# Mixer outputs split into high and low parts where they are produced, and the residual added by an identity product on TensorE instead of an addition on GpSimd

## Chip, cores and metric

One core of a Trainium2 chip runs the whole program. The metric is device time in microseconds (us): the median of several runs. TensorE is called PE, VectorE DVE, ScalarE ACT, GpSimd POOL; SP is the engine that issues nearly all DMAs.

## What is computed

One layer of a streaming encoder over 1024 frames of width 1024. Four mixers, each with 256 output channels, share one input projection. Their outputs are concatenated, multiplied by `w_out` and added to the residual `h`, which is `x` here. A gated feed-forward network, a gated embedding and a last norm follow. The reference, cut to the part that the change touches:

```python
hn = rms_norm(h, norm_mix_g[i])
z_a, z_b, z_c, z_d = _split(hn @ w_in[i], [A_COLS, B_COLS, C_COLS, D_COLS])
o_a = gmlp_spatial_gating(z_a, ...)
o_b = gated_deltanet(z_b, ...)
o_c = rwkv7_time_mix(z_c, ...)
o_d = conformer_conv(z_d, ...)
h = h + jnp.concatenate([o_a, o_b, o_c, o_d], axis=-1) @ w_out[i]
```

## The kernel before, in words

Large products are made in three pieces. Each float32 operand is split into a high part (a cast to fp32r) and a low part (the operand less its high part), and `mm3` (L136) adds high times high, high times low and low times high in PSUM. A split is an ACT cast (L109) and a subtraction (L112) on DVE, or on POOL for most weights.

The engines' orders are not written out by hand. The Tile framework schedules the instructions by a priority (`tc.cur_priority`) and by the costs it assumes, and fixes one static order for each engine and for SP's queue. An engine takes its instructions in that order: one that waits holds up all behind it.

The stages, by the profile's time, are these. Up to about 205 us come the conformer input and convolution, the gMLP input, and the deltanet inputs (`deltanet_prep`). `gmlp_mix` writes the gMLP output `u` to DRAM as `d_oa`, and `conformer_act` writes the conformer output `cod` as `d_od`, both in float32. Up to about 255 us runs `deltanet_pass1`, a loop over 8 tiles of 128 frames. It is followed by `invert`, a serial chain of small DVE operations (L216 and L220, tiles `X` and `Xt`) that inverts 32x32 blocks, until 291 us. Then come the block products (`blocks`, L1146 and L1148), the 8 deltanet tiles and the preparation of the RWKV mixer. Projections (`mps<-hT,wh`) fill PE in between.

From 440 us the RWKV mixer makes its own matrices (L1025; `LT`, `rCd`), a second `invert` runs on DVE until 493 us, two transposes (L1135, L1137, output `Tn`) follow, and then the block products again. Next come 8 RWKV tiles (`rwkv_tiles`) in a software pipeline. For tile t the operations are L1057 to L1112 and L1166, then the state chain (L867, L884), the transposed output (L1122), the product with `w_out` (`osch`, `oscl`) and the norm for the feed-forward network (L161).

`wout_early` is the low-priority work that PE does beside this. For each tile t of 128 frames it loads the outputs of conformer (m=3) and gMLP (m=0) from DRAM as `oaf`, splits each into `osph` and `ospl` (L109 on ACT, L112 on DVE, at the highest priority, three buffers), and makes for each half of the 1024 columns one PSUM sum of 12 products. This is the staged part. ACT copies the sum into `stg` (L423), and POOL adds the whole tile to `h` (L425), where `x` was loaded. There are 8 such tiles, so 192 staged products and 8 POOL additions of 128x1024. The same is done for deltanet (m=1, 96 products) with a DVE addition instead (L427). The weights of m=1 and m=2 take over the buffers of m=3 and m=0, so the product of any RWKV tile with `w_out` follows the end of the staged part.

Of the kernel before, what the change touches and what calls it, by code (L numbers as in the profile page):

```python
# [9 lines left out]
F32 = mybir.dt.float32  # L10
F32R = mybir.dt.float32r
BF16 = mybir.dt.bfloat16
AF = mybir.ActivationFunctionType
ALU = mybir.AluOpType
# [3 lines left out]
P = 128  # L18
S = 1024
D = 1024  # L20
# [77 lines left out]
class Net:  # L98
# [125 lines left out]
    def body(self):  # L224
        tc, nc, I = self.tc, self.nc, self.i
# [18 lines left out]
            self.eps[v] = e  # L244
        dr = ex.enter_context(tc.tile_pool(name="dr", bufs=1, space=bass.MemoryType.DRAM))
        dt = lambda n, k: dr.tile([P, 2 * k, S], F32, name=n)
        self.d_oa, self.d_ob, self.d_od = dt("d_oa", 1), dt("d_ob", 1), dt("d_od", 1)
        self.d_sg, self.d_c = dt("d_sg", 1), dt("d_c", 3)
        self.d_g = dt("d_g", 2)
        self.d_bk = dr.tile([P, 2, NT, 4, 64], F32, name="d_bk")  # L250
# [107 lines left out]
    def wout_early(self):  # L358
        tc, nc, I = self.tc, self.nc, self.i
        self.base = tc.cur_priority  # L360
        tc.cur_priority = self.base + 100000
        for ms in ((3, 0), (1,)):
            if ms[0] == 1:
                tc.cur_priority = self.base + 10000000
            w = [self.wout_load(m, (nc.vector, None if m == 1 else nc.vector), True) for m in ms]
            for t in range(NT):
                ofs = []
                for m in ms:
                    of = self.wo.tile([P, 2, P], F32, name="oaf", tag="oaf", bufs=2)
                    nc.sync.dma_start(out=of, in_=(self.d_oa, self.d_ob, None, self.d_od)[m][:, :, t * P:(t + 1) * P])  # L370
                    ofs.append(of)
                if ms[0] == 3:
                    nc.sync.dma_start(out=self.h[:, t, :], in_=I["x"][t * P:(t + 1) * P, :])
                for _ in self.wout_tile(t, ofs, w, len(ms) == 2):
                    pass
        tc.cur_priority = self.base
# [31 lines left out]
    def wout_tile(self, t, ofs, ws, staged=False, tag="osp", k="h"):  # L408

        nc = self.nc  # L410
        with self.top():
            os = [self.split(of, tag, [P, 2, P], 3 if tag == "osp" else 2, self.wo if tag == "osp" else self.p2) for of in ofs]
        for half in range(2):
            cs = slice(half * 512, half * 512 + 512)
            ps = self.mps(k)
            n = 2 * len(ofs)
            for j in range(n):
                (oh, ol), w = os[j // 2], ws[j // 2][j % 2]
                self.mm3(ps, oh[:, j % 2, :], ol[:, j % 2, :], w[0][:, cs], w[1][:, cs], j == 0, j == n - 1)
            if staged:  # L420
                if half == 0:
                    stg = self.wo.tile([P, D], F32, name="stg", tag="nxn", bufs=1)
                nc.scalar.copy(out=stg[:, cs], in_=ps)  # L423
                if half == 1:
                    nc.gpsimd.tensor_tensor(out=self.h[:, t, :], in0=stg, in1=self.h[:, t, :], op=ALU.add)  # L425
            else:
                nc.vector.tensor_tensor(out=self.h[:, t, cs], in0=ps, in1=self.h[:, t, cs], op=ALU.add)  # L427
            yield
# [68 lines left out]
    def gmlp_mix(self, u, v_tok, ws, bs):  # L497
        nc = self.nc
        for pr in range(2):
            for half in range(2):  # L500
                ps = self.mps()
                for q in range(4):
                    for hp in range(2):
                        h = 2 * pr + hp
                        nc.tensor.matmul(ps[64 * hp:64 * hp + 64, q * P:(q + 1) * P], v_tok[half][:, q, h * 64:(h + 1) * 64],
                                         ws[:, h, :], start=True, stop=True)
                cs = slice(half * 512, half * 512 + 512)
                t1 = self.dt("gt", [P, 4, P])
                nc.vector.tensor_tensor(out=t1, in0=ps.rearrange("p (n i) -> p n i", i=P),
                                        in1=bs[:, pr:pr + 1, :].broadcast_to([P, 4, P]), op=ALU.add)  # L510
                nc.vector.tensor_tensor(out=u[pr][:, cs], in0=u[pr][:, cs], in1=t1.rearrange("p n i -> p (n i)"), op=ALU.mult)
            nc.sync.dma_start(out=self.d_oa[:, pr, :], in_=u[pr])

    def conformer_in(self):
        tc, nc, I = self.tc, self.nc, self.i
# [43 lines left out]
    def conformer_conv(self, gls):  # L559
# [9 lines left out]
            y.append(yc)  # L569
        return y  # L570

    def conformer_out(self, y, yt, t0):
        nc, I = self.nc, self.i
        for t2 in range(t0, t0 + 2):
            ps = self.mps("a")
            for a in range(2):
                t = 2 * t2 + a
                for c in range(2):
                    nc.tensor.transpose(ps[:, a * 256 + c * P:a * 256 + (c + 1) * P], y[c][:, t * P:(t + 1) * P], self.ident)
            yt.append(self.dt("cyt", [P, 2, G]))  # L580
            self.layernorm_tok(self.ar, ps.rearrange("p (a g) -> p a g", a=2), 2, G, 1e-5, yt[-1])

    def conformer_act(self, yt):
        nc = self.nc
        for c in range(2):
            o = self.dt("cod")
            for half in range(2):
                ps = self.mps("a")
                for q in range(4):
                    t = half * 4 + q  # L590
                    nc.tensor.transpose(ps[:, q * P:(q + 1) * P], yt[t // 2][:, t % 2, c * P:(c + 1) * P], self.ident)
                cs = slice(half * 512, half * 512 + 512)
                nc.scalar.activation(out=o[:, cs], in_=ps, func=AF.Silu, scale=self.prm("cflg", c), bias=self.prm("cflb", c))
            nc.sync.dma_start(out=self.d_od[:, c, :], in_=o)

    def deltanet_prep(self, bp, qp, between):
        tc, nc, I = self.tc, self.nc, self.i
# [1046 lines left out]
```

## Time and profile before

| what | value |
|---|---|
| median of 3 runs | 1501.1 us (1489.42 to 1514.49) |
| the profiled execution | 1502.77 us |
| its span, first to last instruction | 1501.0 us |
| mean granted TensorE clock | 0.957 of full speed |
| PE busy | 1404.7 us (94%), 7864 records |
| DVE busy | 1038.3 us (69%) |
| ACT busy | 610.6 us (41%) |
| POOL busy | 480.3 us (32%) |

Busy time is a sum over stages with different limits, so the stages have to be read one by one. A busy PE is not a PE at its peak: the granted clock is either 2.4 GHz (1.0 in the windows) or 1.2 GHz (0.5), and at the lower one the same products take twice the time.

### The profile page before, as it was taken

To read this page: it belongs to the slowest core of one execution; us is meant where nothing else is said; L and a number is where in the kernel's file an instruction comes from. 1 tells how busy PE (TensorE), PEld (TensorE's weight loads), DVE (VectorE), ACT (ScalarE), POOL (GpSimd) and SP (SyncE) were. 2 spreads that over 40 slices of the span, in tenths; PEclk is the share of its full clock that TensorE was granted. 3 is DMA by queue.
4 is the path that set the end of the run, shared out by engine and by line. 5 is a ranking of instruction groups with operands and counts; after the bars stand their busy time and mean duration, and the time that the engine had idled before them with its cause. 6 is when DMAs were issued, how large, how long until landed. Compare 5 with 4: busy or idle time off the path is not lost.

```text
span 1501.0 us, 21081 instructions
## 1 busy us (share of the span) xinstructions
PE 1404.7 (94%) x7864; PEld 1121.0 (75%) x7864; DVE 1038.3 (69%) x1765; ACT 610.6 (41%) x1003; POOL 480.3 (32%) x436
## 2 busy tenths in 40 slices
PE   7996999899997898999789999999999999999997
PEld 6885777677665685777567888888888778877785
DVE  5699866876489538677669666676666695677643
ACT  6342365122543223344544333333333334445544
POOL 3215235172322214122622222222222344484000
PEclk9998999899999659999899999999999999999999
DMA  5100113131146313223453223333332794375032
GB/s 220 62 29 28 60 53 128 57 102 51 66 174 216 108 45 112 75 82 127 127 174 132 100 99 105 105 105 106 105 105 92 251 306 139 97 223 184 29 113 84
DMA packets 91734, 171.77 MB, mean 114 GB/s; under 512 B 12400, under 2 KB 41712, under 8 KB 91376
## 3 DMA queue, kind: packets, MB, share of 16 engines
q1 hardware_dynamic: 91344, 169.93, 34.1%
q8 instruction: 62, 1.02, 0.3%
q10 hardware_dynamic: 288, 0.49, 0.1%
q14 instruction: 40, 0.33, 0.1%
HBM read 120.85 MB, written 49.55 MB: 114 GB/s over the span
## 4 chain that ended last, share of the span: by engine, by line
PE 42%; DVE 3%; issue 3%; POOL 2%; DMA 2%; ACT 2%; SPq 0%; DVEq 0%; POOLq 0%; ACTq 0%
PE pf L136 39%; POOL wl L1215 1%; DMA w<-in_wd 1%; PE mps L136 1%; DVE w L1211 1%; PE px L136 1%; DVE wl L1215 1%; DVE t L1211 0%; ACT wh L1214 0%; DVE s L1211 0%; PE pf L1557 0%; DMA raw<-in_wg 0%; POOL t L1211 0%; DMA early<-in_wd 0%; POOL xT1l L1215 0%
## 5 line engine op out<-in xcount | busy, mean ns | idle before, releaser
L136 PE MATMUL mps<-hT,wh 128*128 128x512 f32 (+1 forms) x736 | 238.9, 404 | 3.0 <-DVE mix L195 2.6
L136 PEld LDWEIGHTS mps<-hT,wh 128*128 128x128 f32 x736 | 138.6, 194 | 35.9 <-DVE mix L195 3.0
L136 PE MATMUL mps<-hT,wl 128*128 128x512 f32 (+1 forms) x368 | 147.0, 399 | 3.8 <-POOL wl L112 3.8
L1215 POOL TENSOR_TENSOR wl<-yr,wh 128x512 fp32r<-128x512 f32 x73 | 106.5, 1464 | 95.4 <-ACT wh L1214 85.6
L136 PE MATMUL pf<-wl,wh 128*128 128x512 f32 x300 | 117.6, 392 | 3.8 <-DVE wl L1215 3.7
L112 POOL TENSOR_TENSOR wl<-raw,wh 128x1024 fp32r<-128x1024 f32 x25 | 64.6, 2588 | 171.2 <-ACT wh L109 171.2
L136 PE MATMUL pf<-wh 128*128 128x512 f32 x300 | 117.0, 390 | 2.0 <-ACT wh L1214 2.0
L136 PE MATMUL pf<-wh,wl 128*128 128x512 f32 x300 | 116.8, 389 | 0.0
L1211 DVE TENSOR_TENSOR pf<-pf,u 128x512 f32<-128x512 f32 x88 | 61.1, 694 | 70.6 <-PE pf L136 70.5
L1214 ACT CAST fq<-s 128x512 fp32r<-128x512 f32 x88 | 53.6, 621 | 121.9 <-PE pf L136 96.8
L1215 POOL TENSOR_TENSOR fq<-raw,fq 128x512 fp32r<-128x512 f32 (+1 forms) x31 | 50.3, 1622 | 152.9 <-ACT fq L1214 152.9
L1215 DVE TENSOR_TENSOR wl<-w,wh 128x512 fp32r<-128x512 f32 x62 | 70.2, 1138 | 37.0 <-ACT wh L1214 37.0
L567 DVE SCALAR_TENSOR_TENSOR cy<-csg,prmt,cy 128x1023 f32<-128x1023 f32 (+29 forms) x60 | 86.4, 1464 | 7.2 <-ACT cy L564 6.6
L136 PEld LDWEIGHTS mps<-hT,wl 128*128 128x128 f32 x368 | 71.5, 194 | 20.1 <-POOL wl L112 4.4
L1215 POOL TENSOR_TENSOR wl<-raw,wh 128x1024 fp32r<-128x1024 f32 (+1 forms) x17 | 40.4, 2379 | 138.8 <-issue 116.6
L1214 ACT CAST wh<-yr 128x512 fp32r<-128x512 f32 x73 | 45.2, 621 | 79.1 <-POOL wl L1215 50.3
L136 PEld LDWEIGHTS pf<-wl,wh 128*128 128x128 f32 x300 | 56.3, 188 | 18.1 <-DVE wl L1215 6.8
L1215 DVE TENSOR_TENSOR fq<-s,fq 128x512 fp32r<-128x512 f32 x66 | 45.6, 693 | 31.7 <-ACT fq L1214 31.7
L136 PEld LDWEIGHTS pf<-wh 128*128 128x128 f32 x300 | 56.2, 188 | 14.1 <-ACT wh L1214 2.4
L136 PE MATMUL pf<-xT2h,fq 128*128 128x512 f32 x176 | 61.0, 408 | 5.2 <-ACT fq L1214 5.2
L136 PEld LDWEIGHTS pf<-wh,wl 128*128 128x128 f32 x300 | 56.3, 188 | 11.6
L109 ACT CAST wh<-raw 128x1024 fp32r<-128x1024 f32 x30 | 31.5, 1050 | 71.8 <-PE mps L136 37.5
(486 smaller groups left out, 3659.3 us busy)
## 6 DMA issues: line engine op xcount, KB each, us to landing
yr<-d_y SPq DMA_DIRECT2D x73, 256.0 KB, 3.2
w<-in_wd SPq DMA_DIRECT2D x55, 256.0 KB, 4.5
raw<-in_wg SPq DMA_DIRECT2D x24, 512.0 KB, 3.6
raw<-in_wu SPq DMA_DIRECT2D x24, 512.0 KB, 3.5
raw<-in_win SPq DMA_DIRECT2D x22, 512.0 KB, 3.8
d_y<-fy SPq DMA_DIRECT2D x11, 512.0 KB, 3.3
d_y<-ys SPq DMA_DIRECT2D x11, 512.0 KB, 3.2
d_y<-ys SPq DMA_DIRECT2D x22, 256.0 KB, 3.7
```

The lines of the kernel that those rows point to most:

```text
L109: self.nc.scalar.copy(out=hi, in_=raw)
L112: (eng or self.nc.vector).tensor_sub(out=lo, in0=raw, in1=hi.bitcast(F32))
L136: mm = lambda *a, **k: self.nc.tensor.matmul(*a, skip_group_check=more, **k)
L567: nc.vector.scalar_tensor_tensor(out=yc[:, sh:], in0=gl[:, 0:S - sh], scalar=self.prm("cfw", 2 * j + c), in1=yc[:, sh:], op0=ALU.mult, op1 ...
L1211: eng.tensor_tensor(out=out, in0=a, in1=b, op=op)
L1214: self.nc.scalar.copy(out=hi, in_=raw)
L1215: eng.tensor_sub(out=lo, in0=raw, in1=hi.bitcast(F32))
```

## The change

Three things are edited. First, the gMLP and conformer outputs are split at the place where they are produced: `store_parts` makes the high part with one ACT cast of 128x1024 and the low part in place with one DVE subtraction, and stores both (four casts, four subtractions, eight stores in place of four). Second, the staged part loads high and low parts ready made into `osph` and `ospl`, with no split left there; only deltanet (m=1) keeps `oaf` and the split. Third, each staged PSUM sum begins with a product of the identity matrix with the `h` tile (both float32), so that ACT copies the finished sum straight into `h`; `stg` and the POOL addition go.

```diff
-        self.d_oa, self.d_ob, self.d_od = dt("d_oa", 1), dt("d_ob", 1), dt("d_od", 1)
+        self.d_ob = dt("d_ob", 1)
+        self.d_oa, self.d_od = [dr.tile([P, 2, 2, S], F32, name=n) for n in ("d_oa", "d_od")]
...
                 for m in ms:
-                    of = self.wo.tile([P, 2, P], F32, name="oaf", tag="oaf", bufs=2)
-                    nc.sync.dma_start(out=of, in_=(self.d_oa, self.d_ob, None, self.d_od)[m][:, :, t * P:(t + 1) * P])
+                    if m == 1:
+                        of = self.wo.tile([P, 2, P], F32, name="oaf", tag="oaf", bufs=2)
+                        nc.sync.dma_start(out=of, in_=self.d_ob[:, :, ts])
+                    else:
+                        of = [self.wo.tile([P, 2, P], F32R, name="osp" + q, tag="osp" + q, bufs=3) for q in "hl"]
+                        for q in range(2):
+                            nc.sync.dma_start(out=of[q].bitcast(F32), in_=(self.d_od if m else self.d_oa)[:, q, :, ts])
                     ofs.append(of)
...
-        with self.top():
-            os = [self.split(of, tag, [P, 2, P], 3 if tag == "osp" else 2, self.wo if tag == "osp" else self.p2) for of in ofs]
+        os = ofs
+        if not staged:
+            with self.top():
+                os = [self.split(of, tag, [P, 2, P], 3 if tag == "osp" else 2, self.wo if tag == "osp" else self.p2) for of in ofs]
         for half in range(2):
...
+            if staged:
+                nc.tensor.matmul(ps, self.ident, self.h[:, t, cs], start=True, stop=False)
             for j in range(n):
                 (oh, ol), w = os[j // 2], ws[j // 2][j % 2]
-                self.mm3(ps, oh[:, j % 2, :], ol[:, j % 2, :], w[0][:, cs], w[1][:, cs], j == 0, j == n - 1)
+                self.mm3(ps, oh[:, j % 2, :], ol[:, j % 2, :], w[0][:, cs], w[1][:, cs], j == 0 and not staged, j == n - 1)
             if staged:
-                if half == 0:
-                    stg = self.wo.tile([P, D], F32, name="stg", tag="nxn", bufs=1)
-                nc.scalar.copy(out=stg[:, cs], in_=ps)
-                if half == 1:
-                    nc.gpsimd.tensor_tensor(out=self.h[:, t, :], in0=stg, in1=self.h[:, t, :], op=ALU.add)
+                nc.scalar.copy(out=self.h[:, t, cs], in_=ps)
...
-            nc.sync.dma_start(out=self.d_oa[:, pr, :], in_=u[pr])
+            self.store_parts(self.d_oa, pr, u[pr])
...
+    def store_parts(self, dst, c, x):
+        nc = self.nc
+        hi, lo = self.dt("oh", None, F32R), x.bitcast(F32R)
+        nc.scalar.copy(out=hi, in_=x)
+        nc.vector.tensor_sub(out=lo, in0=x, in1=hi.bitcast(F32))
+        nc.sync.dma_start(out=dst[:, 0, c, :], in_=hi.bitcast(F32))
+        nc.sync.dma_start(out=dst[:, 1, c, :], in_=x)
...
-            nc.sync.dma_start(out=self.d_od[:, c, :], in_=o)
+            self.store_parts(self.d_od, c, o)
```

The scheduler makes a new order of the whole program from this, and it differs beyond the edited lines. Line numbers after the edited places are higher by 16 in the changed kernel. Three places of the order follow.

POOL from the RWKV matrices to the memsets for the RWKV tiles (`LT`, `rMo` belong to the matrices, `sbd` tiles to the RWKV tiles), before:

```order
L1182 TENSOR_SCALAR rMo_3661<-LT 32x128 x8
L1182 TENSOR_SCALAR rMo_3662<-LT 32x128 x8
L425 TENSOR_TENSOR h<-stg,h 128x1024 x5
L1201 MEMSET sbdZ_5047 128x1024
L1201 MEMSET sbdZ_5048 128x1024
L1201 MEMSET sbdE_5051 128x512
```

The same place on POOL in the changed kernel:

```order
L1198 TENSOR_SCALAR rMo_3677<-LT 32x128 x8
L1198 TENSOR_SCALAR rMo_3678<-LT 32x128 x8
L1217 MEMSET sbdZ_5031 128x1024
L1217 MEMSET sbdZ_5032 128x1024
L1217 MEMSET sbdE_5035 128x512
```

The five additions of the stretch of the second inversion are gone from POOL, and so are the three that stood later.

PE at the end of the staged products that stand ahead of the block products (`Tn`, `rMo`, `rTc`: results of the inversion), before:

```order
L136 MATMUL mps<-wh,ospl 128x512
L1146 MATMUL mps<-Tn,rMo_3661 32x32 x32
L136 MATMUL mps<-wh,osph 128x512
L136 MATMUL mps<-wl,osph 128x512
L136 MATMUL mps<-wh,ospl 128x512
L1148 MATMUL mps<-rTc,Q 32x32 x32
L1146 MATMUL mps<-Tn,rMo_3662 32x32 x32
```

The same place on PE in the changed kernel:

```order
L136 MATMUL mps<-wh,ospl 128x512
L427 MATMUL mps<-h,ident 128x512
L1162 MATMUL mps<-Tn,rMo_3677 32x32 x32
L136 MATMUL mps<-wh,osph 128x512
L136 MATMUL mps<-wl,osph 128x512
L136 MATMUL mps<-wh,ospl 128x512
L1164 MATMUL mps<-rTc,Q 32x32 x32
L1162 MATMUL mps<-Tn,rMo_3678 32x32 x32
```

Between the last product of the RWKV matrices and the first block product PE had 8 projections and 129 products of `osph` and `ospl`; it now has 72 of them and 7 identity products. From there to the last L884 of RWKV tile 2 it had 55 and now has 41 and 3 identity products; from there to the first norm transposes (L161) 47, now 127 and 6 identity products; after that 57, now 48. The 29 projections that stood among and behind the products L1025 now stand earlier.

ACT where the conformer output is made and `deltanet_pass1` begins (`cod` the conformer output, `kq` and `dq` tiles of pass 1, `bsg` a deltanet gate), before:

```order
L686 ACTIVATE bsg<-mps 128x512
L109 CAST wh<-raw 128x1024
L593 ACTIVATE cod<-mps,prmt 128x512 x2
L710 COPY kq<-mps 128x512
L720 ACT_TABLE_LOAD
L720 ACTIVATE dq<-dq 128x256
L727 COPY dq<-mps 128x256
```

The same place on ACT in the changed kernel:

```order
L583 CAST oh<-cod 128x1024
L609 ACTIVATE cod<-mps,prmt 128x512 x2
L726 COPY kq<-mps 128x512
L583 CAST oh<-cod 128x1024
L736 ACT_TABLE_LOAD
L736 ACTIVATE dq<-dq 128x256
L743 COPY dq<-mps 128x256
L726 COPY kq<-mps 128x512
L702 ACT_TABLE_LOAD
L702 ACTIVATE bsg<-mps 128x512
L736 ACT_TABLE_LOAD
L736 ACTIVATE dq<-dq 128x256
```

Two casts stand ahead of the first exponential of pass 1 (L736), and a gate with its own function table now stands between the first and the second, which brings two more table loads. On PE, 18 projections moved into the first tiles of pass 1.

## Rows read from the trace of the kernel before

**Rows 1.** The page, 40 equal slices of 37.5 us: granted TensorE clock in tenths.
```profile
PEclk9998999899999659999899999999999999999999
```

**Rows 2.** Busy time by stretch: window, length, engines busy (records), granted clock, DMA.
```profile
454.00:498.60 44.60, 32.88 (x130) 24.48 (x128) 43.50 (x138) 12.02 (x23) 12.17 (x5) 0.95 0.51 171
498.60:577.00 78.40, 74.91 (x670) 58.97 (x671) 34.12 (x96) 19.70 (x44) 20.34 (x40) 0.63 0.25 74
577.00:599.20 22.20, 17.19 (x62) 12.43 (x62) 18.24 (x35) 7.61 (x14) 11.09 (x5) 0.85 0.51 165
599.20:703.60 104.40, 102.59 (x824) 79.79 (x824) 72.75 (x206) 40.16 (x90) 18.19 (x31) 1.00 0.26 89
...
518.00:563.00 45.00, 44.05 (x266) 35.15 (x267) 13.81 (x43) 9.90 (x24) 6.25 (x18) 0.51 0.24 71
```

**Rows 3.** Waits of PE from 454 to 600: total us, times, longest us.
```profile
PE mps L136 <- DVE ospl L112: 5.5, 2, 3.6
PE mps L1146 <- DVE Tn L1137: 3.4, 1, 3.4
PE mps L1122 <- DVE oloc L469: 3.0, 2, 1.7
PE mps L136 <- DVE wl L112: 2.9, 2, 1.9
...
PE mps L1078 <- DVE rAA L1071: 1.4, 1, 1.4
```

**Rows 4.** Timeline of DVE in the second inversion: start us, us, operation, count.
```profile
463.58 2.49 DVE L216 TENSOR_TENSOR Xt<-rCs,X 128x84 f32<-128x84 f32 x2
466.00 0.40 DVE L220 TENSOR_TENSOR X<-X,Xt 128x84 f32<-128x84 f32 x2
468.80 2.63 DVE L216 TENSOR_TENSOR Xt<-rCs,X 128x110 f32<-128x110 f32 x2
...
478.95 2.49 DVE L220 TENSOR_TENSOR X<-X,Xt 128x126 f32<-128x126 f32 x1
...
484.67 2.58 DVE L216 TENSOR_TENSOR Xt<-rCs,X 128x92 f32<-128x92 f32 x2
...
495.35 1.24 DVE L112 TENSOR_TENSOR ospl<-oaf,osph 128x256 fp32r<-128x256 f32 x1
```

**Rows 5.** Timeline of POOL in the same stretch.
```profile
463.41 2.40 POOL L425 TENSOR_TENSOR h<-stg,h 128x1024 f32<-128x1024 f32 x1 [11.15 <-ACT stg L423]
...
484.76 2.36 POOL L425 TENSOR_TENSOR h<-stg,h 128x1024 f32<-128x1024 f32 x1 [3.46 <-ACT stg L423]
```

**Rows 6.** The tile `oaf`: its instructions (min/median/max ns) and its loads.
```profile
L112 DVE TENSOR_TENSOR ospl<-oaf,osph x24: 414/424/2498, 426.5 to 616.8; 128x256 fp32r<-128x256 f32 x24
L370 SPq DMA_DIRECT2D oaf<-d_od x8: 518/526/580, 423.4 to 496.6; - x8
...
DMA to landing us min/median/max: 2.4/2.7/4.8
```

**Rows 7.** Timeline of PE: float32 products, then split ones at either clock.
```profile
437.33 1.91 PE L1007 MATMUL mps<-mix,cst 128*128 128x512 f32 x4
438.68 0.80 PE L136 MATMUL mps<-hT,wh 128*128 128x512 f32 x1
...
461.50 0.39 PE L136 MATMUL mps<-wh,ospl 128*128 128x512 f32 x1
461.73 0.39 PE L136 MATMUL mps<-wh,osph 128*128 128x512 f32 x1
...
488.58 0.63 PE L136 MATMUL mps<-wl,osph 128*128 128x512 f32 x1
489.00 0.63 PE L136 MATMUL mps<-wh,ospl 128*128 128x512 f32 x1
```

**Rows 8.** Timeline of ACT at the start of pass 1.
```profile
227.93 1.04 ACT L109 CAST wh<-raw 128x1024 fp32r<-128x1024 f32 x1
...
230.81 1.28 ACT L720 ACT_TABLE_LOAD   x1
```

More of the change, by code (lines that the diff above doesn't have):

```diff
@@ L367, in wout_early @@
                 ofs = []
+                ts = slice(t * P, (t + 1) * P)
                 for m in ms:
-                    of = self.wo.tile([P, 2, P], F32, name="oaf", tag="oaf", bufs=2)
-                    nc.sync.dma_start(out=of, in_=(self.d_oa, self.d_ob, None, self.d_od)[m][:, :, t * P:(t + 1) * P])
+                    if m == 1:
[5 more added lines that the diff above has]
+                            nc.sync.dma_start(out=of[q].bitcast(F32), in_=(self.d_od if m else self.d_oa)[:, q, :, ts])
                     ofs.append(of)
                 if ms[0] == 3:
-                    nc.sync.dma_start(out=self.h[:, t, :], in_=I["x"][t * P:(t + 1) * P, :])
+                    nc.sync.dma_start(out=self.h[:, t, :], in_=I["x"][ts, :])
                 for _ in self.wout_tile(t, ofs, w, len(ms) == 2):
```

## The prediction

> **What bounds the kernel now.** I read the page first, for the clock by slices; then the windows by stage; then the waits and timelines of the stretch in which the staged products run. The page's line of granted clocks is near full speed everywhere but in two neighbouring slices, about 488 to 563 us [rows 1]. So the stretch that the change rearranges is also the one at half clock. The windows cut it at the places that the order names [rows 2]. Up to 498.6 us, where `Tn` ends, DVE is busy for 43.50 of 44.60 us and PE for 32.88: DVE sets the pace, and PE fills its gaps with staged products. From 498.6 to 577 PE is busy for 74.91 of 78.4 us at a clock of 0.63, and in its core, 518 to 563, for 44.05 of 45 us at 0.51. Up to 599.2 come the leftover products, from there to 703.6 the pipelined RWKV tiles, with PE busy for 102.59 of 104.4 us at full clock. Hence the rule that I use: before `Tn` a microsecond counts on DVE and is free on PE; behind `Tn` it counts on PE.
>
> PE's waits say the same. Before `Tn` it waits for splits (5.5 and 2.9 us) and for `Tn` itself (3.4), 11.8 in all [rows 3]. On DVE four steps of the inversion take 2.49 to 2.63 us where an undisturbed pair takes 0.40 [rows 4]. Two of them coincide with POOL additions of 2.40 and 2.36 us that started 0.17 us earlier at 463.41 and 0.09 us later at 484.76 [rows 5]. I therefore put all four down to the POOL additions, five of which lie in this stretch.
>
> **The prices.** A split on DVE is 0.42 us [rows 6]; consecutive DVE instructions overlap by 0.07 us (463.58 + 2.49 against 466.00 [rows 4]), so one that goes gives 0.35. A staged product is 0.23 us at full clock (461.50 to 461.73) and 0.42 at half (488.58 to 489.00). The identity product is float32, and its nearest row is L1007 of the same shape: that row starts at 437.33 and holds two products as the order lists them; the product behind it starts at 438.68 and lasts 0.80 in place of 0.39, so PE came free near 439.09, and 1.76 / 2 = 0.88 us is one product [rows 7]. At half clock I take 1.76. The lower bound is 0.23, if it runs like a split product; the upper 1.91, if the row's whole length is one.
>
> **The sum, in order of time.** It is made against the profiled execution, 1502.8 us, which is 1.7 above the median of the runs.
>
> Start of pass 1: **+4.6**. The order puts two ACT casts of 128x1024 ahead of the first exponential and brings two more function table loads: 2 x 1.04 + 2 x 1.28 [rows 8]. I take ACT as pacing this place. The bounds are 0, since the 18 projections that moved in here (4.2 us of PE work) are gone from where PE was wanted later, and +8, if the two DVE subtractions count too (1.7 each, four times a split of 128x256). The casts and subtractions of the gMLP output I cost at nothing: they lie beside the convolution's products on PE, and without that cover they would be the same two casts and two subtractions, 5.5 us.
>
> DVE up to `Tn`: **-14.0**. Without POOL additions the four stalled steps give 2.09 + 2.23 + 2.09 + 2.18 = 8.6 us [rows 4]. Of the 24 splits, 16 go; 13 of those stood ahead of `Tn`. Twelve give 0.35 each, 4.2; the one at 495.35 took 1.24 and gives 1.2. The least I allow is -5.4 (the splits alone, if something else on POOL stalls the same steps); more than 14 has no row. PE must do its part inside the shorter stretch: 72 products at 0.23 (16.6) and 7 identity products at 0.88 (6.2) are 22.8 us in some 44.6 - 14 = 30.6. They are hidden by DVE's chain; without that cover they cost up to 6.2. POOL's memsets for the RWKV tiles now follow directly on `rMo` and may lie beside the inversion. No row shows a DVE step beside one: the bounds are 0 and +4.4, a stall like those above for each of the two memsets of 128x1024 (2 x 2.2), and I take 0, because the stalls that I can pair with POOL work have additions beside them. The page "SBUF — State Buffer" of the Trainium skill, section "Who interferes with whom", says that a DVE operation with two SBUF inputs contends with a POOL instruction that reads SBUF and not with one that only writes it; the two paired stalls agree with its first half, and by its second half the memsets cost 0, not 4.4.
>
> From `Tn` to the last L884 of tile 2, at half clock: **-3.3**. 14 products fewer (55 to 41) are -5.9, 3 identity products at 1.76 are +5.3, and two waits for DVE that I put down to the POOL additions left in this stretch, 1.4 for `rAA` and the shorter 1.3 for `oloc` [rows 3], go.
>
> From there to the first norm transposes: **+20.0**. 80 products more (47 to 127) are +18.4 and 6 identity products +5.3. The wait for `oloc` of 1.7 goes. The clock here was 0.85 over 22.2 us [rows 2], that is about 6.7 us at half clock, worth at most 3.3; with PE working all through I take 2.0 of it back. This is the largest term. It can't hide: the weights of m=1 and m=2 take the buffers of the staged part, so the tiles wait until it has ended.
>
> Tiles 3 to 7: 9 products fewer (57 to 48) on a full PE, **-2.1**.
>
> 4.6 - 14.0 - 3.3 + 20.0 - 2.1 = +5.2, so **1508 us**. In short, DVE's chain ends earlier, and the products that PE did in its shade are done behind it. All 16 identity products would cost 14.1 us at full clock; of the additions that they replace POOL had no need. What else changes is hidden: ACT loses 16 splitting casts and gains four larger ones; SP issues 16 more loads of 0.53 us [rows 6] where its queue has room; 2 MB more each way is little beside a DMA share of at most 0.51 [rows 2].
>
> **Rivals.** First, *the gain stays*. If the casts at pass 1 are hidden (-4.6) and the shorter, steadier stretch before `Tn` keeps the clock up, the 45 us at 0.51 with 44.05 us of PE work shrink by up to 22; of that I take 15: 1508 - 4.6 - 15 = **1488**. For it: PE's long waits for splits (longest 3.6 us) stood just where the clock fell, products being 0.42 apart at 488.58, and those splits are gone. Against it: the wait for `Tn` remains, and the block products after it are many small ones.
>
> Second, *the loads become the wait*, the slower side. High and low parts now come straight from DRAM into three buffers each. A buffer comes free after 18 of a tile's 24 products, and the next tile but one needs it 12 products and one identity product later: 12 x 0.23 + 0.88 = 3.6 us. In that time two issues of 0.53 and a landing of 2.7 have to pass, 3.8 us, and with the longest landing, 4.8, some 5.9 [rows 6]: a gap of up to 2.3 for each of the last five tiles, about 10 us. It decides when landings exceed some 2.6 us, or SP holds a load back behind others. If such gaps also drop the clock in the fill stretch, 42 us of PE work (22.2 + 20.0) at half speed lose another 20 or so: 1508 + 10 + 20 = **1538**. For it: the clock did fall after waits of a few microseconds [rows 1, 3]. Against it: the parts of a tile are needed one after the other, and the splits that lay between landing and product are gone. The Trainium skill's page "TensorE: Matmul & The Clock Gate", section "HAM oscillation — how this bites in real kernels", describes just this: bursts of products between waits for DMA fall back to half clock again and again; that speaks against the change, and by it this rival's second half comes true.
>
> A third, that the edit doesn't do what it says, has no room: the order shows POOL without additions and PE with 16 identity products. Only their price is open: the nine that count, 10.6 us in the sum, would be 2.7 at 0.23 (three of them at 0.42), a time of 1500, and 22.9 at 1.91 (three at 3.82), a time of 1520.
>
> **How the numbers follow.** The forecast has 0.64, with a range of its own of 1495 to 1520 from the bounds of the identity product, the casts and DVE's chain. The first rival has 0.20, the second 0.10, and 0.06 is left for a different order of waits. A difference of 2%, 30 us, is about what a measurement of this kernel can tell from no change. The first rival is 13 us faster and only with the full 22 of the clock and a cheap identity product passes 30, so faster has 0.06; slower is the second rival, 0.10; the same 0.84. The range goes from 1484 to 1534, leaving out half of the second rival and the tip of the first.
>
> **What would show it.** In the changed profile, 32 or fewer records of the identity product, with PE free again 0.88 us after each, and `Tn` some 9 us earlier than 498.6 (4.6 later by pass 1, 14 sooner by DVE) with no inversion step near 2.5 us; a POOL without the additions; a clock of 0.5 still behind `Tn`; and the first norm transposes 7 us later than before. It is wrong if inversion steps still take 2.5 us, if PE waits for `osph` or `ospl` on a DMA by more than a microsecond a tile, if the clock stays at 1.0 behind `Tn`, or if two table loads more at pass 1 delay nothing.

## Result and the profile after

| | before | changed kernel |
|---|---|---|
| median, 14 runs each | 1492.67 us (1486.49 to 1514.49) | 1502.57 us (1498.41 to 1512.35) |
| ratio, 95% interval | | 1.0073 (1.0048 to 1.0097) |
| profiled execution, span | 1502.77 us, 1501.0 us | 1499.13 us, 1497.3 us |
| mean granted clock in it | 0.957 | 0.967 |

The change costs 0.7%, some 10 to 11 us; 1508 us had been forecast, 5.2 more than the profiled execution of before. The two profiled executions alone would show a gain of 3.6 us, and they must not be read against each other, because the time goes with the mean granted clock. Of 35 later runs of before, 20 with a clock of 0.964 or more took 1487 to 1500 us and 15 with 0.956 or less took 1503 to 1517 us. Of the changed kernel's 14 runs, seven with 0.965 or more took 1498 to 1501 us and seven with 0.962 or less took 1504 to 1512 us. The profile shown ahead of the prediction has the lower clock, that of the changed kernel the higher one. So the comparison stage by stage uses a second profile of before with the higher clock (1488.89 us, span 1487.1 us, clock 0.968). The ratio leaves out slow runs, which here is one of before (1514.49 us) and none of the changed kernel; with it the means are 1495.1 and 1503.8 us, 8.7 apart.

The page's granted clock in 40 slices, the changed kernel first, then the second profile of before. Both lack the pair of slices at 0.6 and 0.5 of [rows 1].

```profile
PEclk9998999979998799999899999999999999999999
```

```profile
PEclk9998999989999799999999999999999999999999
```

The windows of the stages of [rows 2]: up to the end of `Tn`, to the last L884 of tile 2, to the first norm transposes, and tiles 3 to 7. The columns are those of [rows 2]: window, length, busy time of PE, PEld, DVE, ACT and POOL (records), granted clock, DMA share, GB/s. The second profile of before:

```profile
457.90:502.50 44.60, 30.99 (x126) 23.30 (x126) 43.76 (x137) 10.90 (x22) 12.70 (x5) 0.95 0.51 170
502.50:562.20 59.70, 56.66 (x670) 44.61 (x670) 33.90 (x95) 19.53 (x44) 20.33 (x40) 0.87 0.33 97
562.20:584.80 22.60, 17.52 (x62) 12.75 (x62) 17.84 (x35) 7.59 (x14) 11.08 (x5) 0.85 0.51 162
584.80:689.20 104.40, 102.60 (x825) 79.90 (x825) 72.81 (x206) 40.10 (x91) 18.11 (x31) 1.00 0.26 89
```

The changed kernel:

```profile
452.20:496.80 44.60, 34.13 (x211) 22.97 (x210) 42.86 (x162) 10.02 (x25) 5.87 (x16) 0.86 0.67 232
496.80:552.50 55.70, 55.52 (x663) 43.10 (x664) 29.39 (x93) 15.81 (x37) 15.39 (x38) 0.87 0.34 103
552.50:592.30 39.80, 38.30 (x154) 27.98 (x153) 17.84 (x37) 12.18 (x23) 7.95 (x4) 1.00 0.42 131
592.30:698.00 105.70, 101.76 (x821) 78.73 (x819) 72.05 (x204) 40.28 (x92) 19.22 (x32) 1.00 0.25 88
```

The reader is to compare lengths and ends. `Tn` ends 5.7 us earlier (502.5 to 496.8), and the stretch behind it is 4.0 shorter (59.7 to 55.7) at the same clock of 0.87. Then the leftover products take 39.8 us in place of 22.6, +17.2, with PE busy for 38.30. Tiles 3 to 7 are 1.3 longer, and what follows (1487.1 - 689.2 against 1497.3 - 698.0) is 1.4 longer: -5.7 - 4.0 + 17.2 + 1.3 + 1.4 = +10.2, which is the difference of the two spans.

Ahead of `Tn`, landmarks of DVE's timeline divide the -5.7: the small memset (L206) that precedes the first step of each inversion. The second profile of before, then the changed kernel:

```profile
260.27 0.09 DVE L206 MEMSET X<- 128x32 f32 x1
...
461.50 0.09 DVE L206 MEMSET X<- 128x32 f32 x1
```

```profile
262.33 0.09 DVE L206 MEMSET X<- 128x32 f32 x1
...
470.33 0.09 DVE L206 MEMSET X<- 128x32 f32 x1
```

The first inversion starts at 260.3 and 262.3 (+2.1; the first profile of before had 257.4, so +2 to +5), the second at 461.5 and 470.3 (another +6.8), and from there to the end of `Tn` it takes 41.0 and 26.5 (-14.5). Whether +2 or +5 is right is settled by a landmark on ACT just ahead of pass 1, the first output of the conformer, again before (second profile) and changed:

```profile
228.96 1.45 ACT L593 ACTIVATE cod<-mps,prmt 128x512 f32<-128x512 f32 x2
```

```profile
226.90 1.45 ACT L609 ACTIVATE cod<-mps,prmt 128x512 f32<-128x512 f32 x2
```

From there to the first inversion it is 31.3 us in both profiles of before (226.08 to 257.37 in the first) and 35.4 in the changed kernel: +4.1. The other 2 us lie ahead of this landmark, where the two profiles of before themselves differ by 2.9.

DVE's timeline in the changed kernel's second inversion, the answer to [rows 4] (start, us, operation, count). No step takes 2.5 us any more; the widest pairs take 0.49, and between the 23 us of steps stands no split.

```profile
474.16 0.41 DVE L216 TENSOR_TENSOR Xt<-rCs,X 128x84 f32<-128x84 f32 x2
...
482.41 0.49 DVE L216 TENSOR_TENSOR Xt<-rCs,X 128x119 f32<-128x119 f32 x2
...
494.91 1.87 DVE L1153 STREAM_TRANSPOSE Tn<-X 128x1024 f32<-128x1024 f32 x1
```

PE's waits in the changed kernel from 452 to 600, the answer to [rows 3] (engine, line, releaser, total us, times, longest). The waits for splits, for `rAA` and for `oloc` are gone. PE now waits 5.8 us for `Tn`, and 0.6 for a tile of `x`. Its products wait for no load of `osph` or `ospl`.

```profile
PE mps L1162 <- DVE Tn L1153: 5.8, 1, 5.8
PE mps L1041 <- ACT LT L1043: 2.3, 4, 0.8
PE mps L1041 <- DVE bk L1003: 1.9, 1, 1.9
...
PE mps L427 <- DMA h<-in_x: 0.6, 1, 0.6
```

PE's timeline in the changed kernel: the last identity product ahead of `Tn`, the first block product behind it with the idle time ahead of it, then one identity product of the fill stretch with the products that follow.

```profile
490.10 1.02 PE L427 MATMUL mps<-h,ident 128*128 128x512 f32 x2
...
496.93 1.92 PE L1162 MATMUL mps<-Tn,rMo 32*32 32x32 f32 x64 [5.81 <-DVE Tn L1153]
...
561.43 1.02 PE L427 MATMUL mps<-h,ident 128*128 128x512 f32 x2
...
561.88 0.80 PE L136 MATMUL mps<-wh,osph 128*128 128x512 f32 x1
...
562.52 0.39 PE L136 MATMUL mps<-wl,osph 128*128 128x512 f32 x1
```

The price comes out as in [rows 7]: the identity product starts at 561.43, the third product at 562.52, and with 0.23 for the second the identity product occupies PE for 562.52 - 0.23 - 561.43 = 0.86 us (0.88 forecast).

ACT's timeline at the start of pass 1, the answer to [rows 8]: two casts, and two more loads of a function table around one gate.

```profile
229.68 1.05 ACT L583 CAST oh<-cod 128x1024 fp32r<-128x1024 f32 x1
...
232.43 1.07 ACT L583 CAST oh<-cod 128x1024 fp32r<-128x1024 f32 x1
233.52 1.28 ACT L736 ACT_TABLE_LOAD   x1
...
236.32 1.28 ACT L702 ACT_TABLE_LOAD   x1
...
238.23 1.28 ACT L736 ACT_TABLE_LOAD   x1
```

### The profile page after: what moved, and what is told of

Its sections match the earlier page's. It is cut to its first block, busy times and chain, and to the rows that moved or that the text cites. A ratio compares the mean times of both kernels' runs of the same rounds, so it can differ in the third digit from the quotient of the medians.

```text
span 1497.3 us, 21129 instructions
## 1 busy us (share of the span) xinstructions
PE 1401.1 (94%) x7896; PEld 1116.6 (75%) x7896; DVE 1029.5 (69%) x1753; ACT 609.5 (41%) x993; POOL 462.6 (31%) x428
## 4 chain that ended last, share of the span: by engine, by line
PE 60%; DVE 16%; issue 6%; ACT 5%; POOL 4%; DMA 3%; SPq 0%; POOLq 0%; ACTq 0%; DVEq 0%
PE pf L136 37%; PE mps L136 9%; DVE cy L574 2%; DVE Xt L216 2%; DMA w<-in_wd 2%; DVE X L220 1%; POOL wl L1231 1%; DVE wl L1231 1%; DVE w L1227 1%; PE px L136 1%; PE mps L1086 1%; DVE by L195 1%; PE mps L1182 1%; PE mps L883 1%; PE mps L942 1%
## 5 line engine op out<-in xcount | busy, mean ns | idle before, releaser
L136 PE MATMUL mps<-hT,wh 128*128 128x512 f32 (+1 forms) x736 | 235.9, 401 | 5.0 <-DVE mix L195 4.6
L109 ACT CAST wh<-raw 128x1024 fp32r<-128x1024 f32 x30 | 31.3, 1048 | 75.5 <-PE mps L136 37.0
```

The source lines that it names most:

```text
L109: self.nc.scalar.copy(out=hi, in_=raw)
L136: mm = lambda *a, **k: self.nc.tensor.matmul(*a, skip_group_check=more, **k)
```

## Experiments

Every kernel was timed beside runs of before on its chip; the ratio is to these.

**1. Before once more.**

> The kernel before, once more, for a second profile of it. Its 14 runs go from 1486 to 1514 us, so a profile can fall on either end. Theory: the runs differ by the TensorE clock behind Tn; a profile near 1489 has a half-clock spell behind Tn of some 20 us or less in place of the 45 us of the first profile, and up to Tn the same times within 2 us. Rival: the runs differ at many places by small amounts, and the spell behind Tn is there in each of them.

Measured: 1491.43 us (12 runs), ratio 0.9989 (0.9953 to 1.0024). The theory holds but for one figure. Behind `Tn` the stretch to the last L884 of tile 2 takes 59.7 us at a clock of 0.87, where [rows 2] had 78.4 at 0.63, and this alone (18.7) is more than the 13.9 us by which the spans differ; `Tn` itself ended 4.0 us later than in the first profile, outside the 2 us expected. So most of the 14 us between these two executions is the clock behind `Tn`, with one and the same program.

**2. Only the early split.** `stg` and the POOL addition are put back into the changed kernel:

```diff
-            if staged:
-                nc.tensor.matmul(ps, self.ident, self.h[:, t, cs], start=True, stop=False)
...
-                nc.scalar.copy(out=self.h[:, t, cs], in_=ps)
+                if half == 0:
+                    stg = self.wo.tile([P, D], F32, name="stg", tag="nxn", bufs=1)
+                nc.scalar.copy(out=stg[:, cs], in_=ps)
+                if half == 1:
+                    nc.gpsimd.tensor_tensor(out=self.h[:, t, :], in0=stg, in1=self.h[:, t, :], op=ALU.add)
```

> The changed kernel with stg and the GpSimd addition put back, so only the outputs are split early. Theory (the sum of the prediction with the sizes measured since): start of pass 1 +7, DVE chain up to Tn only -5.4 (splits gone, stalls of about 2.1 us in the inversion back), 14 products fewer behind Tn -3: between -2 and +2 us of before. Rival (the early split is what makes the changed kernel slower): +8 to +11 us, since the second inversion starts 10 us later and PE behind Tn gives nothing back.

Measured: 1498.24 us (12 runs, 1494.65 to 1500.77), ratio 1.0016 (0.9983 to 1.005). By the ratio the theory stands and the rival's +8 to +11 is out. But all these runs have a clock of 0.964 or more, and not all those of before have; against the 20 of before with such a clock (median 1491.8) they are 6.4 us longer, between the two. Profile against profile at about the same clock (0.965 and 0.968) the span is 9.9 us longer (1497.0), and the second inversion starts 13.8 us later (475.3): the rival's description. DVE's timeline and POOL's in the inversion settle another point:

```profile
475.92 2.50 DVE L216 TENSOR_TENSOR Xt<-rCs,X 128x30 f32<-128x30 f32 x2
...
481.64 2.61 DVE L220 TENSOR_TENSOR X<-X,Xt 128x84 f32<-128x84 f32 x2
...
487.53 2.53 DVE L216 TENSOR_TENSOR Xt<-rCs,X 128x120 f32<-128x120 f32 x2
...
493.42 2.69 DVE L220 TENSOR_TENSOR X<-X,Xt 128x128 f32<-128x128 f32 x2
```

```profile
475.88 2.39 POOL L434 TENSOR_TENSOR h<-stg,h 128x1024 f32<-128x1024 f32 x1 [3.54 <-ACT stg L432]
...
481.45 2.52 POOL L434 TENSOR_TENSOR h<-stg,h 128x1024 f32<-128x1024 f32 x1 [3.18 <-ACT stg L432]
...
487.04 2.69 POOL L434 TENSOR_TENSOR h<-stg,h 128x1024 f32<-128x1024 f32 x1 [3.06 <-ACT stg L432]
...
493.41 2.55 POOL L434 TENSOR_TENSOR h<-stg,h 128x1024 f32<-128x1024 f32 x1 [3.69 <-DMA osph<-d_oa]
```

Four steps take 2.5 to 2.7 us, each starting within 0.5 us of the start of one of four POOL additions, with no split in the inversion. So the four stalls of [rows 4], of which the prediction paired only two, are the additions'. POOL's timeline of the first profile of before has the other two as well, which [rows 5] leaves out; they go with the steps at 468.80 and 478.95:

```profile
468.93 2.37 POOL L425 TENSOR_TENSOR h<-stg,h 128x1024 f32<-128x1024 f32 x1 [3.12 <-ACT stg L423]
478.63 2.67 POOL L425 TENSOR_TENSOR h<-stg,h 128x1024 f32<-128x1024 f32 x1 [7.34 <-ACT stg L423]
```

**3. Only the identity product.** The kernel before with the change's two edits to the sum (identity product first, ACT copy into `h`), and splits where they were.

> The kernel before with the identity product and the copy into h, splits left where they were. Theory: pass 1 as before (0), the four inversion steps lose their 2.1 us (-8.6), behind Tn 58 products more (+13), 9 identity products more (+8 to +11), waits for DVE and the half-clock bit in the fill stretch gone (-6), 9 products fewer at the end (-2): +4 to +8 us. Rival (the early split is what costs): 0 or a few us faster than before.

Measured: 1493.7 us (12 runs), ratio 0.9987 (0.9957 to 1.0017); its span is 7.1 us longer than that of the second profile of before, its runs 1486 to 1498. The theory's +4 to +8 is out and the rival's 0 stands. None of these runs has a clock under 0.966, as many of before have; against those of before with 0.964 or more (median 1491.8) it is 1.9 us behind, which runs with such a spread can't tell from nothing. Its inversion and `Tn` take 28.9 us (465.5 to 494.4), 12.1 less than before, and 80 staged products stand ahead of `Tn` in the order where before has 129. PE's waits from 452 to 500 give a reason that the change's own profile shows with only 0.6 us:

```profile
PE mps L1144 <- DVE Tn L1135: 3.9, 1, 3.9
PE mps L418 <- DMA h<-in_x: 3.7, 1, 3.7
```

A sum that begins with the identity product can't begin before its tile of `x` has landed (run 9 shows the other case).

**4 and 5. The conformer's casts at lower priority.** All else is the changed kernel's.

```diff
+        self.late = []
...
-            self.store_parts(self.d_od, c, o)
+            self.late.append((c, o))
+        base, self.tc.cur_priority = self.tc.cur_priority, self.tc.cur_priority + 5000
+        for c, o in self.late:
+            self.store_parts(self.d_od, c, o)
+        self.tc.cur_priority = base
```

> The changed kernel with the casts and subtractions of the conformer output at a lower priority, behind the first copies of pass 1; the gate bsg no longer stands between two exponentials, so the two extra function table loads are gone, and 14 of the 17 projections go back. Theory: the first inversion starts 4 to 6 us earlier than in the changed kernel, and all of it stays: 4 to 6 us less than the changed kernel, some 5 more than before. Rival (what is lost at pass 1 is hidden by PE's later work): the same time as the changed kernel within 2 us.

Measured: 1496.55 us (12 runs), ratio 0.999 (0.9953 to 1.0028): level with before, where 5 us more had been expected. The first inversion starts at 260.3, 2.0 us earlier than in the changed kernel and not 4 to 6. Then, on one chip, the changed kernel and this one:

> The changed kernel once more, on the chip of the next three runs. Theory (the early split of the conformer output costs some 5 us at pass 1 and 4 us by 17 projections moved to where PE has no room, and the kernel before has runs with and without a long half-clock spell behind Tn): 1498 to 1510 us, 6 to 12 more than the runs of before whose mean clock is 0.964 or more. Rival (the first comparison was a matter of the chip): as before within 3 us.

> The changed kernel with the conformer's casts at lower priority, for a comparison on one chip. Theory: 4 to 10 us less than the changed kernel beside it, its second inversion starting some 7 us earlier. Rival (the gain is hidden by what PE does later): within 2 us of it.

Measured: the changed kernel 1507.07 us (12 runs), ratio 1.0069 (1.004 to 1.0098), so the loss is not a matter of the chip; late casts 1498.86 us (12 runs), ratio 1.0008 (0.9981 to 1.0034). The theory holds: 8.2 us less, with the second inversion starting at 463.7 in place of 471.2. Of these 7.5 us, 2.1 are there at the first inversion (260.8 and 262.9), and 5.4 come between the two. From the conformer's first output to the first inversion all four profiles with late casts (runs 4, 5, 8 and 10) take 32.4 us, all four with the change's casts (both of the changed kernel, runs 2 and 9) 35.4 to 35.5, and the six without an early split 31.3: the casts and loads at pass 1 cost 4.1 us, and lower priority gives 3.1 of them back. The two extra table loads are gone from ACT's timeline. Of the 29 projections that the changed kernel has more than before ahead of the RWKV matrices, the trace with late casts has 6 left, all of them in pass 1 (the expectation's 14 of 17 don't come out of the traces).

The runs on this chip also show where the changed kernel's loss lies. With a clock of 0.964 or more its median is 1500.9 us (5 runs) and that of before 1493.0 (18 runs), +7.9; with a lower one 1509.9 (7 of its 12 runs) and 1508.4 (10 of the 28 of before), +1.5. So a part of the loss is that more of its runs have the lower clock.

**6 and 7. DVE adds from PSUM.** The kernel before, with neither POOL addition nor identity product:

```diff
-            if staged:
-                if half == 0:
-                    stg = self.wo.tile([P, D], F32, name="stg", tag="nxn", bufs=1)
-                nc.scalar.copy(out=stg[:, cs], in_=ps)
-                if half == 1:
-                    nc.gpsimd.tensor_tensor(out=self.h[:, t, :], in0=stg, in1=self.h[:, t, :], op=ALU.add)
-            else:
-                nc.vector.tensor_tensor(out=self.h[:, t, cs], in0=ps, in1=self.h[:, t, cs], op=ALU.add)
+            nc.vector.tensor_tensor(out=self.h[:, t, cs], in0=ps, in1=self.h[:, t, cs], op=ALU.add)
```

> The kernel before with the staged sums added to h by DVE straight from PSUM: no GpSimd addition, no stg, no identity product. Theory (only the shared stalls, the added PE work and the products left for behind Tn count): stalls gone (-8.6), 12 additions of 128x512 in the inversion at some 0.65 us (+8), so Tn within 1 us of before; 34 products more ahead of Tn and 43 fewer between Tn and the first norm transposes (-10), 9 more after (+2): 5 to 9 us faster than good runs of before. Rival (what is moved ahead of Tn makes PE late for the first block products): no faster than before.

> The fastest version so far once more, for more runs of it on the chip of the other two. Theory: 1470 to 1480 us, 1.0 to 1.9% less than before. Rival (six runs were luck): less than 0.7% from before.

Measured: 1474.84 us (6 runs), ratio 0.9851 (0.9813 to 0.989), and 1477.5 us (6 runs), ratio 0.9879 (0.9841 to 0.9917): faster than both given kernels, by more than was expected in the first and as expected in the second. The window that ends with `Tn`, as long as that of the other kernels, and the one from there to the first norm transposes:

```profile
456.70:501.30 44.60, 40.49 (x167) 31.50 (x166) 43.05 (x157) 8.24 (x17) 0.11 (x1) 0.98 0.54 183
501.30:562.00 60.70, 57.76 (x676) 45.13 (x676) 39.37 (x104) 21.51 (x46) 22.35 (x41) 0.92 0.45 140
```

DVE is as full as before (43.05 of 44.6 us) and `Tn` no earlier (501.3). But PE is busy for 40.49 us in place of 30.99, and the first norm transposes come at 562.0, 22.8 us earlier than in the second profile of before (run 7: 566.4, 18.4 earlier). The theory had 10 us for the products moved ahead of `Tn`. The windows name most of the rest: from `Tn` to the norm transposes PE stands idle for 2.9 us in place of 8.1, and the clock is 0.92 in place of 0.87 and 0.85, by an estimate worth up to 6. That neither was tried by itself leaves their shares open.

**8. Late casts and DVE additions.** The changed kernel with the edits of 4 and of 6.

> The changed kernel with late conformer casts and DVE additions from PSUM in place of the identity products. Theory: as the run before it, but the inversion is 12 splits shorter (-4) and 24 fewer products lie behind Tn than in before (-6), less 2 for the late casts: 5 to 12 us faster than good runs of before, and faster than both given kernels. Rival (loads of ready parts or the clock decide): no faster than before.

Measured: 1481.63 us (11 runs), ratio 0.9906 (0.9878 to 0.9935): faster than both given kernels, but some 4 to 7 us behind 6 and 7, which keep the splits late. The early split gave nothing that can be seen here.

**9. The identity product last.**

```diff
-            if staged:
-                nc.tensor.matmul(ps, self.ident, self.h[:, t, cs], start=True, stop=False)
...
-                self.mm3(ps, oh[:, j % 2, :], ol[:, j % 2, :], w[0][:, cs], w[1][:, cs], j == 0 and not staged, j == n - 1)
+                self.mm3(ps, oh[:, j % 2, :], ol[:, j % 2, :], w[0][:, cs], w[1][:, cs], j == 0, j == n - 1 and not staged)
             if staged:
+                nc.tensor.matmul(ps, self.ident, self.h[:, t, cs], start=False, stop=True)
```

> The changed kernel with the identity product as the last of each staged sum instead of the first, so that a sum can begin before its tile of x has landed; its price is the same, and the order puts 102 products ahead of Tn in place of 72. Theory (what the change loses behind Tn is staged products that are left for there, 0.23 us each): 35 to 43 products fewer between Tn and the first norm transposes (-8 to -10), 9 more after (+2): 5 to 9 us faster than the changed kernel. Rival (the identity products themselves, 0.87 us each, are the loss): the same as the changed kernel within 2 us, since there are 16 of them still.

Measured: 1484.99 us (10 runs, 1483.76 to 1488.43), ratio 0.9936 (0.9916 to 0.9956). The 16 identity products are still there, and against the changed kernel's 1.0073 and 1.0069 the time falls by 1.3%, some 20 us (14.7 from profile to profile). The rival is out, and the gain is more than the theory's 5 to 9. The windows of the four stages:

```profile
454.00:498.60 44.60, 38.99 (x241) 25.33 (x239) 42.64 (x162) 10.44 (x26) 5.57 (x16) 1.00 0.71 239
498.60:551.40 52.80, 52.00 (x667) 39.69 (x668) 29.73 (x94) 16.46 (x38) 15.35 (x38) 0.97 0.40 120
551.40:579.10 27.70, 26.04 (x104) 18.50 (x102) 16.69 (x35) 10.73 (x19) 7.97 (x4) 1.00 0.45 143
579.10:683.60 104.50, 102.75 (x826) 79.99 (x825) 72.86 (x206) 40.13 (x91) 18.15 (x31) 1.00 0.26 90
```

`Tn` ends 1.8 us later than in the changed kernel, yet PE is busy for 38.99 us ahead of it in place of 34.13. The fill stretch takes 27.7 us in place of 39.8 (-12.1). The clock behind `Tn` is 0.97 in place of 0.87, and that stretch is 2.9 shorter. The span is 14.7 us shorter (1482.6). By the trace 106 staged products stand ahead of `Tn` in place of 72, and 43 fewer between `Tn` and the first norm transposes (34 went ahead of `Tn`, 9 behind the transposes), 10 us at 0.23; the clock, 0.10 more over 55.7 us, is by an estimate worth up to 5.6.

Why more sums stand ahead is seen where they begin. In the changed kernel the first staged sum begins at 465.42, set free by the landing of the first tile of `x`. In this run the first staged product starts at 449.62, and the first tile of `x` is issued at 462.14 only, by SP's timeline. PE's timeline in the changed kernel, then here:

```profile
465.42 2.08 PE L427 MATMUL mps<-h,ident 128*128 128x512 f32 x2 [0.58 <-DMA h<-in_x]
```

```profile
449.62 0.40 PE L136 MATMUL mps<-wh,osph 128*128 128x512 f32 x1
```

**10. Both mends.** The edits of 4 and 9.

> Both mends together: conformer casts at lower priority, identity product last. Theory: the two gains add, -7 and -7 from the changed kernel: 1485 to 1493 us, level with good runs of before and still some 10 us behind the version with DVE additions. Rival (one of them hides the other): no faster than the run with late casts alone.

Measured: 1478.93 us (6 runs), ratio 0.9901 (0.987 to 0.9932). The two gains add, and to more than expected.

**11. The identity product last, splits late in the program.** The kernel before with the identity product as in 9.

> The kernel before with the identity product as last of each staged sum and no early split: what the early split is worth once the rest is mended. Theory (12 splits of 0.35 us in the inversion are all that the early split saves, and with late casts it costs little): 2 to 6 us slower than the version with both mends, 1480 to 1486 us. Rival (the early split is worth nothing or costs, as it did beside the DVE additions): the same or faster than that version, under 1479 us.

Measured: 1480.64 us (6 runs, 1475.26 to 1490.46), ratio 0.9883 (0.9813 to 0.9954). This does not tell the two apart from run 10: the intervals overlap. With the rest mended, no worth of the early split can be seen.

## Why the prediction came out as it did

The direction, the range and the main mechanism were right; the forecast change, +5.2 us, was half of the measured 10 to 11. That 1508 came as near as 5 us to the measured 1502.6 is luck in part: it was built on a profiled execution of 1502.8, 10 us above the median of before in the 14 runs, and the change was 5 too small, two misses that work against each other. Step by step, against the second profile of before:

| step | forecast | measured |
|---|---|---|
| ahead of the conformer's first output | 0 | -2.1, less than the 2.9 between the two profiles of before |
| from there to the first inversion (pass 1) | +4.6 | +4.1 |
| from the first inversion to the second | no term | +6.8 |
| DVE from there up to `Tn` | -14.0 | -14.5 |
| to the last L884 of tile 2 | -3.3 | -4.0 |
| fill stretch | +20.0 | +17.2 |
| tiles 3 to 7 | -2.1 | +1.3 |
| the rest | 0 | +1.4 |

*To the last L884 of tile 2* the sum was made at half clock. The two profiles have that only for the first part of the stretch (0.50 from 502.5 to 518 in before, from 496.8 to 511 in the changed kernel), and 0.87 in the mean. At the prices of full clock the sum gives -3.3 as well (-3.2 + 2.6 - 2.7), so the agreement doesn't test the price.

*DVE up to `Tn`* was right in size and in cause: the stalls are the POOL additions' (run 2), and they went. The identity products stayed hidden there; PE even stood idle for 5.8 us ahead of `Tn`, time for 25 staged products that a fixed order had put behind it.

*The fill stretch* was the largest term and right in kind: 80 products and 6 identity products on a PE that is busy throughout. It was 2.8 too large, and not by the identity product's price (0.86 for 0.88). By the windows PE's idle time fell by 3.6 us (5.1 to 1.5) where the forecast had taken off 1.7, and the clock rose from 0.85 over 22.6 us to 1.00, worth up to 3.4 where 2.0 had been taken off; the two together cover the 2.8. Run 9 shows the mechanism by undoing it: it has 43 products fewer between `Tn` and the first norm transposes, and the stretch shrinks by 12.1 us.

*The step that failed* is one that the sum doesn't have: it goes from the start of pass 1 straight to the second inversion and puts the 200 us between the two inversions at nothing. The only word on it is the lower bound of 0 for pass 1, because the 18 projections moved in there "are gone from where PE was wanted later". Measured, this stretch is 6.8 us longer (201.2 to 208.0), in two parts.

The first inversion itself, from its memset to the end of its `Tn`, takes 36.7 us in place of 34.0. One more POOL operation now falls on one of its steps, the low part of a weight; DVE's timeline, then POOL's, in the changed kernel:

```profile
287.57 2.51 DVE L216 TENSOR_TENSOR Xt<-Cs,X 128x96 f32<-128x96 f32 x2
```

```profile
287.23 2.57 POOL L112 TENSOR_TENSOR wl<-raw,wh 128x1024 fp32r<-128x1024 f32 x1 [11.82 <-ACT wh L109]
```

The same third stall is there in runs 2 to 5 and 7 to 10 (36.0 to 36.8 us) and not in before, run 6 or run 11 (34.0), so it needs no early split. Runs 6 and 7 are the same kernel and differ in it.

From there to the second inversion it takes 171.4 us in place of 167.2. Over all profiles this is 171.4 to 174.6 with the change's casts (both of the changed kernel, runs 2 and 9) and 166.9 to 167.4 with late casts, in before and in run 11. So it goes with the early casts, and late casts undo it. That the moved projections are the cause is not shown: runs 3, 6 and 7, with every projection where before has it, take 169.6 to 170.4. These three share with the changed kernel a lower clock from the first `Tn` to the RWKV matrices (0.92 to 0.93, where before, the late casts and run 11 have 0.94). How much is this clock, and how much the 8 more projections that stand in that stretch by the trace (1.8 us at 0.23), was not tried and stays open.

*Tiles 3 to 7* came out with the wrong sign, by a small amount. PE's busy time there fell by 0.8 us (102.60 to 101.76) and not by 2.1, and one wait was added. PE's waits from 592 to 698 in the changed kernel, of which before has 0.4 us in place of the 2.0:

```profile
PE mps L136 <- POOL wl L1231: 2.0, 1, 2.0
```

*The rivals.* The first, a clock that stays up, looks confirmed by [rows 2] against the changed kernel's windows and is not: a better clock behind `Tn` is there in the kernel before as well (run 1), at the same 0.87. The forecast's own sign, a clock of 0.5 behind `Tn`, is there for some 14 us in the changed kernel's profile, not for the 45 us of [rows 2]; its runs with the lower clock (1504 to 1512 us) were not profiled, and what happens in them stays open. The second, waits for the loaded parts, did not come: the parts land after a median of 2.9 us in the changed kernel, yet one weight load waits for them, 0.5 us, and no product. The Trainium skill's "TensorE: Matmul & The Clock Gate", section "HAM oscillation — how this bites in real kernels", tells of bursts of products between waits for DMA; it had next to nothing to work on here, where PE's waits for DMA from 452 to 600 us are this one and 0.6 us for `x`. The landings and the wait, from the tile's view:

```profile
L377 SPq DMA_DIRECT2D osph<-d_od x8: 359/372/552, 423.8 to 561.4; - x8
...
  DMA osph<-d_oa: 0.5, 1
...
DMA to landing us min/median/max: 2.1/2.9/4.7
```

*The memsets* at a price of 0 were not put to the test: in the changed kernel POOL ran them from 507.8 us on, behind the inversion. The 4.4 us of the other bound and the second half of the rule in the Trainium skill's "SBUF — State Buffer", section "Who interferes with whom", are both left unshown; run 2 agrees with its first half, four times over.

## What to carry to other kernels

Where a fixed order puts filler work beside a serial chain, the value of an edit is set by how much filler the new order leaves for later: here 9 identity products behind `Tn` were worth less than the 43 staged products that went with the identity product's place in the sum. An operand that lands late belongs at the end of a PSUM sum, as runs 9 to 11 have it, and not at its start. Read from the order of every engine what was moved into which stage before pricing it at nothing. And before two profiles are compared, see whether their granted clocks are alike, and compare stretches between landmarks rather than times from the start.

## What the runs showed that was not expected

- The same program takes 59.7 us at a clock of 0.87 or 78.4 at 0.63 for the same stretch behind `Tn`, and this makes most of the 14 us between its two profiles.
- Moving one product from the first place of a sum to the last, with the same instructions in a new order, took 1.3% off the time (1.0073 and 1.0069 to 0.9936, each against before on its chip), and all ten runs lie between 1483.8 and 1488.4 us.
- The plainest addition did as well as any: `h` plus PSUM on DVE, 12 times 0.68 us inside the very chain that sets the pace, left `Tn` where it was and gave 1.2 to 1.5% over before. Its medians are the lowest, but the intervals overlap with those of runs 10 and 11.
